# GpSimd in place of VectorE for the forward substitution in the 16x16 diagonal blocks of the RWKV mixer

## The chip, the cores and the metric

The kernel runs on one core of a Trainium2 chip. The metric is the device time of one execution in microseconds; the time of a version is the median of its runs.

## What is computed

The program runs a first block of three mixers side by side (HGRN2, mLSTM, RWKV7) over 16 meta tokens and 256 tokens of width 2048, and then two layers of a second block. The change lies in the RWKV7 mixer. For each of its 16 heads and each chunk of tokens the reference solves a unit lower triangular system:

```python
def rwkv7_chunk(s_mat, inp):
    ...
    l_ab = jnp.einsum('bhtd,bhsd,bhtsd->bhts', a_, b, d_strict)
    l_ak = jnp.einsum('bhtd,bhsd,bhtsd->bhts', a_, k, d_strict)
    rhs = (jnp.einsum('bhtd,bhdv->bhtv', a_ * jnp.exp(cw_prev), s_mat)
           + jnp.einsum('bhts,bhsv->bhtv', l_ak, v))
    u = lax.linalg.triangular_solve(jnp.eye(length, dtype=rhs.dtype) - l_ab, rhs,
                                    left_side=True, lower=True, unit_diagonal=True)
    ...
    y = (jnp.einsum('bhtd,bhdv->bhtv', r * jnp.exp(cw), s_mat)
         + jnp.einsum('bhts,bhsv->bhtv', r_b, u) + jnp.einsum('bhts,bhsv->bhtv', r_k, v))
```

## The kernel before

**Projections.** Most of the work is the product of the tokens (128 features by up to 272 tokens a tile) with all weight matrices. The helper `unit` streams a weight in pieces of 128 rows by 8 x 128 columns: SyncE's queue issues the DMA into `wraw`; ScalarE rounds the piece to `whi` (L267, by `act`); VectorE makes the remainder `wlo` = `wraw` - `whi` (L270, by `tt`); TensorE runs 24 matmuls into the PSUM tile `pj` (L291): for each of eight sub-tiles `xh` by `whi`, `xl` by `whi` and `xh` by `wlo`. There are four buffers each of `wraw`, `whi` and `wlo` (`self.nraw, self.nhl = 4, 4`), and a buffer is free when its 24 matmuls are done.

**Mixers beside the projections.** The mixers' own work is emitted beside the projections that follow, and has its matmuls in PSUM tiles named `mx`. Each engine runs its instructions in one fixed order; the framework's scheduler sets that order from its own estimates when the program is built (`schedule_with_timeline_sim=True`). What an engine's queue holds behind a waiting instruction waits too.

**The inverse of I - L.** RWKV has four groups of four heads (`front_c`, `back_c`), near 90, 315, 540 and 760 us. In a group:

- TensorE forms `Lb` (for two chunks of 128 tokens) and `Dc` (the meta tokens' part); `base_start` cuts the 16x16 diagonal blocks out of `Lb` on GpSimd (tiles `db`, `Dc`), writes them to memory (`ld`, L621) and reads them back as `LB` (L622), so that each of the 128 partitions holds a row's own block. Both DMAs are issued from GpSimd's queue.
- TensorE computes `vm,Lm` (a matmul of `vm` and `Lm`), ScalarE copies it to `rum`.
- `base_solve` solves all the small blocks at once: `yc` starts as the identity, and 15 steps each multiply a row of `LB` with a column of `yc` into `yt` and add `yt` to `yc`. The operands have 12 x 15 elements per partition in the first step and 12 x 1 in the last; 30 instructions, each of which needs the one before.
- The first reader of `yc` on TensorE is the matmul `rum,yc` (four instructions in the order, eight in the trace). The first on VectorE is `Y<-yc`, with which `inverse` begins for each chunk.

The step in the loop of `base_solve`, on VectorE:

```python
            self.mul(t, self.LB[:, j, :, j + 1:], y[:, :, j:j + 1].to_broadcast([P, 12, 15 - j]))
            self.add(y[:, :, j + 1:], y[:, :, j + 1:], t)
```

Of the kernel before, what the change touches and what calls it, by code (L numbers as in the profile page):

```python
# [13 lines left out]
ALU = mybir.AluOpType  # L14
PSUM = bass.MemoryType.PSUM
DRAM = bass.MemoryType.DRAM

P = 128
# [11 lines left out]
# ---------------------------------------------------------------- host layout  # L30
# [7 lines left out]
def unit_list():  # L38
    """(name, source, width, [(dst column, source column, count)]) in the order the weights are used."""
    u = []  # L40

    def win(name, base, i):
        u.append((f"{name}{i}", "w_in", 256, [(0, W_IN[base] + 256 * i, 256)]))

    u.append(("c_small", "w_in", 164, [(0, W_IN["c_wd"], 128), (128, W_IN["b_ig"], 4), (160, W_IN["b_fg"], 4)]))
    for g in range(4):
        for n in ("c_k", "c_r", "c_v", "c_z"):
            win(n, n, g)
    for g in range(4):
        for n in ("a_f", "a_i", "a_q", "a_z"):  # L50
            win(n, n, g)
    for j in range(8):
        win("g_c", "g_c", j)
        u.append((f"br_c{j}", "w_br2", 256, [(0, 256 * j, 256)]))
    for g in range(2):
        win("b_k", "b_k", g)
        win("b_q", "b_q", g)
        for h in (2 * g, 2 * g + 1):
            for n in ("b_v", "b_o", "b_z"):
                win(n, n, h)  # L60
    for b, s in (("a", "w_br0"), ("b", "w_br1")):
        for j in range(8):
            win(f"g_{b}", f"g_{b}", j)
            u.append((f"br_{b}{j}", s, 256, [(0, 256 * j, 256)]))
    for j in range(8):
        u.append((f"out{j}", "w_out", 256, [(0, 256 * j, 256)]))
    for l in range(2):
        def w2(name, cols, width=256):
            u.append((f"L{l}{name}", f"w_in_2_{l}", width, cols))

        w2("small", [(0, W_IN2["dt"], 32), (32, W_IN2["i_w"], 16), (64, W_IN2["i_k"], 64)], 128)
        w2("a_k", [(0, W_IN2["a_k"], 256)])
        w2("a_v", [(0, W_IN2["a_v"], 256)])
        for j in range(4):
            w2(f"i_q{j}", [(0, W_IN2["i_q"] + 256 * j, 256)])
        for j in range(4):
            w2(f"a_q{j}", [(0, W_IN2["a_q"] + 256 * j, 256)])
        for j in range(4):
            w2(f"a_g{j}", [(0, W_IN2["a_g"] + 256 * j, 256)])
        for g in range(4):  # L80
            w2(f"bc{g}", [(0, W_IN2["bm"] + 128 * g, 128), (128, W_IN2["cm"] + 128 * g, 128)])
            for j in range(2):
                w2(f"xs{2 * g + j}", [(0, W_IN2["xs"] + 512 * g + 256 * j, 256)])
            for j in range(2):
                w2(f"z{2 * g + j}", [(0, W_IN2["z"] + 512 * g + 256 * j, 256)])
        for g in range(4):
            w2(f"pool_v{g}", [(0, W_IN2["pool_v"] + 256 * g, 256)])
            w2(f"pool_g{g}", [(0, W_IN2["pool_g"] + 256 * g, 256)])
        for j in range(8):
            u.append((f"L{l}out{j}", f"w_out_2_{l}", 256, [(0, 256 * j, 256)]))  # L90
    return u
# [12 lines left out]
# per-feature vectors, feature-major: name -> (columns of 128 features)  # L104
# [73 lines left out]
def pack(inp):  # L178
    """Lays the inputs out: weights in the order of their use, vectors feature-major."""
# [58 lines left out]
# ---------------------------------------------------------------- kernel  # L238
class Kernel:
# [5 lines left out]
    # ---- helpers  # L245
# [55 lines left out]
    # ---- weights against the token matrix  # L301
    def unit(self, name, src, cols, evac, chunks=None):
        """evac(j, ps): ps [128, N] = 128 columns of the weight, transposed, times the tokens cols of src (a function of
        the tile and cols that gives the two parts); chunks: the parts of the weight's rows that meet its tiles."""
# [34 lines left out]
    def hot(self):  # L339
        """what frees the PSUM of the projections goes first"""  # L340
        return self.tc.high_priority(offset=self.hprio)
# [13 lines left out]
    def run(self, gen):  # L355
        """Emits a generator and those that it spawns together, each ahead by its own clock."""
# [15 lines left out]
    def early(self, *shape, rows=P, name="r"):  # L372
        """The same, taken now: a slot is taken at the first write, and later ones wait for it."""
        t = f = self.reg(*shape, rows=rows, name=name)
        for _ in shape[1:]:
            f = f[:, 0]
        self.G.memset(f[:, :1], 0.0)
        return t

    def reg(self, *shape, rows=P, name="r"):  # L380
        """A slot of the register file: fp32, at most 544 elements per partition."""
# [15 lines left out]
    def warm_ln(self, late):  # L397
        """has the table of the logarithm loaded before a sum that is waited for; late is what comes just before"""
        self.act(self.warm, late, AF.Ln, scale=0.0, bias=self.eps(2))

    def rstd(self, out, ssum, scale, eps):
        """out = (ssum * scale + eps) ** -0.5"""
# [3 lines left out]
    def follow(self, a, b):  # L406
        """b comes after a in the order of their engine"""
# [3 lines left out]
    # ---- program  # L411
# [37 lines left out]
    def block1(self, b1):  # L449
        nc, tc = self.nc, self.tc  # L450
        xh, xl = self.xh, self.xl
        # the tokens times the weights of the norm; the factors of the norm itself follow the projections
# [27 lines left out]
    def mixers(self, order):  # L480
        """The projections in the given order; the rest of each group runs beside those that follow."""
# [19 lines left out]
    def block1_main(self):  # L501
# [9 lines left out]
        # w_out and the residual, and what the second block's projections take (without its tokens' factors R)  # L511
# [58 lines left out]
    def residual0(self):  # L570
        """the second block's input"""
# [7 lines left out]
    def merge(self, b, y, acc, first):  # L579
        """acc += 2 sigmoid(gate) * (y @ w_br)"""  # L580
# [18 lines left out]
    # ---- RWKV7  # L599
    def lerp(self, out, ps, col):  # L600
        """out = ps + (prev - ps) * mu along the tokens"""
# [8 lines left out]
    def base_start(self, Lb):  # L610
        """the diagonal blocks of 16 of the two chunks' Lb, next to those of the meta tokens, to each of their rows"""
# [13 lines left out]
    def base_solve(self):  # L625
        """rows of ((I - L)^-1)^T in those blocks: 4 heads of each chunk, then of the meta tokens"""
# [3 lines left out]
        for j in range(15):  # L630
            t = tmp[j % 2][:, :, j + 1:]
            self.mul(t, self.LB[:, j, :, j + 1:], y[:, :, j:j + 1].to_broadcast([P, 12, 15 - j]))
            self.add(y[:, :, j + 1:], y[:, :, j + 1:], t)
# [3 lines left out]
    def inverse(self, LT, yc):  # L637
        """Y = ((I - Lm)^-1)^T for four heads; LT [s, 4, t] = Lm^T, strictly upper; yc [s, 4, 16]: Y's diagonal blocks.
        Blocks of twice the size at each level: the lower left of the lower triangular X = Y^T gains X L X."""
# [31 lines left out]
        # blocks of 64 from those of 32; X's second half is not needed any more  # L671
# [33 lines left out]
    def pair(self, K, Q, c, mask, name):  # L705
        """(head i = 2 hh + j sits on the partitions rr of feature tile j)"""
# [11 lines left out]
    def pairm(self, out, K, Q):  # L718
        """the same for the meta tokens"""
# [35 lines left out]
    def front_c(self, g):  # L755
# [7 lines left out]
        # decay and rate  # L763
# [11 lines left out]
        # sums of the decay over each chunk (times -CC is the log)  # L775
# [19 lines left out]
        # S' = exp(cref) S over the chunks  # L795
# [33 lines left out]
        # scaled operands  # L829
# [14 lines left out]
        # token-major b, k  # L844
# [27 lines left out]
        # bonus  # L872
# [9 lines left out]
        # token-major v  # L882
# [17 lines left out]
    def back_c(self, g, ops):  # L900
# [6 lines left out]
        # meta tokens: the state they leave  # L907
# [72 lines left out]
        # layer norm over each head, bonus, gate  # L980
# [17 lines left out]
    # ---- HGRN2  # L998
    def start_a(self):
        p1, P8 = self.p1, [P, 8]  # L1000
        # lower bound of the forget gate: cumsum(softmax over layers) - its first, one layer
# [57 lines left out]
    def back_a(self, g, ops):  # L1059
# [6 lines left out]
        # meta tokens: the state they leave  # L1066
# [20 lines left out]
        # first chunk: the state it leaves  # L1087
# [19 lines left out]
        # scores [s, t]: the diagonal, then pairs by the block where they part, the decay taken from its middle  # L1107
# [64 lines left out]
    # ---- mLSTM  # L1172
    def log1pexp(self, x, rows, n, alloc):
        """log(1 + exp(-|x|)) by its series in e / (2 + e)"""
# [13 lines left out]
    def conv(self, out, ps, off, taps, n, bias=None):  # L1188
        """out[t] = bias + sum_i taps[i] ps[off + t + i - 3], zero before ps"""
# [9 lines left out]
    def silu2(self, t, x):  # L1199
        """x = 2 silu(x) (or into t, for x in PSUM)"""  # L1200
# [77 lines left out]
    def back_b(self, h, k, q, vT, vm, z):  # L1278
# [4 lines left out]
        # log weights [s, t], then the scores  # L1283
# [45 lines left out]
        # layer norm over the head's 256 features  # L1329
# [19 lines left out]
    # ---- block 2  # L1349
    def layer(self, l):  # L1350
# [17 lines left out]
        # w_out: first the SSD features, then pool and attention  # L1368
# [81 lines left out]
    def nrm(self, out, ps, cols=slice(0, T)):  # L1450
        """a projection's result times its tokens' factors"""
        self.mul(out, ps, self.R[:, cols])

    def small2(self):
# [3 lines left out]
        if l == 0:  # L1458
            # halved taps and bias, so that tanh of the convolution is that of its half
# [28 lines left out]
    def back_dt(self, x):  # L1488
        reg, l, nc = self.early, self.l, self.nc
        sm = lambda *shape, name, rows=P: self.p2.tile([rows, *shape], F32, tag="d_" + name, name=name, bufs=1)  # L1490
        # dt, its log decay, and the sums over each chunk: blocks of 16, then the blocks
# [23 lines left out]
        # token-major: [token, chunk, head]  # L1515
# [17 lines left out]
    def rope(self, tmp, x, kind, o, n):  # L1533
        """x (one tile of features, tokens o .. o + n) turned by its position, in place; tmp is zero outside the rows"""
# [15 lines left out]
    def attention(self):  # L1550
# [5 lines left out]
        for j in range(4):  # L1556
# [3 lines left out]
            # each head's two parts above each other  # L1560
# [6 lines left out]
            if j == 0:  # L1567
                # index weights, token-major
# [41 lines left out]
    def back_index(self, qi, ng):  # L1610
        """index scores and the mask of the chosen keys"""
# [107 lines left out]
    def back_ssd(self, g, bc, xs, zs):  # L1719
# [19 lines left out]
        # token-major x dt, and the states after the first two chunks  # L1739
# [127 lines left out]
# ---------------------------------------------------------------- launch  # L1867
# [20 lines left out]
```

## Time and profile before

| | |
|---|---|
| median of three runs | 3028.24 us (3027.68 to 3031.04) |
| span of the profiled execution | 3026.2 us |
| TensorE matmul | 2943.5 us busy (97%) |
| VectorE | 2011.9 us (66%) |
| ScalarE | 1426.1 us (47%) |
| GpSimd | 175.8 us (6%) |

The profiled execution is known by its span; it lies 2.0 us under the median of the timed runs. A group name such as `pj<-xh,whi` gives the tile that is written and those that are read. A busy TensorE is not TensorE at its peak: matmuls are pipelined, so their durations overlap, and the distance from start to start tells the pace. An idle time in brackets lies just before the instruction, with what ended it.

### The profile page before, as it was taken

The page shows a single profiled execution, that of the slowest core. Times are in us where ns is not written, and L with a number is a line of the kernel's source. Part 1 is how long each engine was busy: PE and PEld are TensorE (multiplying, and loading weights), DVE is VectorE, ACT ScalarE, POOL GpSimd, SP SyncE. Part 2 cuts the span into 40 slices and gives each one's busy share as a digit, 9 for nine tenths or more (in the row PEclk, how much of TensorE's full clock was granted, in tenths as well). Part 3 has the DMA queues.
Part 4 walks back from the last instruction along what each step waited for, and adds up shares of the span by engine and source line. Part 5 has one row for each costly group of instructions (what it writes and reads, how often), then busy time and mean ns, then how long its engine had stood idle before and what let it go on. Part 6 is the DMA issues. An engine that isn't in the chain of part 4 may idle for free. (4 is left out here: it accounts for less than half of the span.)

```text
span 3026.2 us, 57135 instructions
## 1 busy us (share of the span) xinstructions
PE 2943.5 (97%) x23566; PEld 2824.0 (93%) x23566; DVE 2011.9 (66%) x3505; ACT 1426.1 (47%) x2041; POOL 175.8 (6%) x324
## 2 busy tenths in 40 slices
PE   8899899899899999999999999999989999999997
PEld 8899899888889999999999899999979999999997
DVE  7657657647545555566976787774568767887655
ACT  6445445435335444456544444443555444544453
POOL 1000100001000000000200000000022000000000
PEclk9999999999999999999999999999989999999999
DMA  6533433433524655556655445555545544555563
GB/s 215 148 109 110 140 105 112 140 99 126 153 91 147 187 183 187 184 186 212 193 167 163 139 152 161 167 177 176 177 158 168 178 152 152 177 174 189 175 183 124
DMA packets 134005, 479.37 MB, mean 158 GB/s; under 512 B 17552, under 2 KB 18064, under 8 KB 133232
## 3 DMA queue, kind: packets, MB, share of 16 engines
q1 hardware_dynamic: 122112, 441.80, 46.8%
q0 software_dynamic: 11200, 32.84, 3.9%
q8 instruction: 184, 3.01, 0.4%
q10 hardware_dynamic: 432, 1.09, 0.1%
q14 instruction: 77, 0.63, 0.1%
HBM read 467.35 MB, written 7.02 MB: 157 GB/s over the span
## 5 line engine op out<-in xcount | busy, mean ns | idle before, releaser
L291 PE MATMUL pj<-xh,whi 128*128 128x272 f32 (+2 forms) x6080 | 1757.7, 289 | 17.1 <-ACT xh L267 15.0
L291 PE MATMUL pj<-xh,wlo 128*128 128x272 f32 (+2 forms) x6080 | 1752.1, 288 | 16.5 <-DVE wlo L270 16.5
L291 PE MATMUL pj<-xl,whi 128*128 128x272 f32 (+2 forms) x6080 | 1749.3, 288 | 7.5 <-DVE xl L288 7.5
L267 ACT ACTIVATE whi<-wraw 128x1024 fp32r<-128x1024 f32 x840 | 887.5, 1057 | 1272.4 <-PE pj L291 1078.3
L270 DVE TENSOR_TENSOR wlo<-wraw,whi 128x1024 fp32r<-128x1024 f32 x840 | 1027.9, 1224 | 558.4 <-ACT whi L267 551.9
L291 PEld LDWEIGHTS pj<-xh,wlo 128*128 128x128 f32 x6080 | 1152.7, 190 | 29.2 <-DVE wlo L270 17.0
L291 PEld LDWEIGHTS pj<-xh,whi 128*128 128x128 f32 x6080 | 1149.0, 189 | 31.0 <-ACT xh L267 15.7
L291 PEld LDWEIGHTS pj<-xl,whi 128*128 128x128 f32 x6080 | 1151.3, 189 | 16.6 <-DVE xl L288 8.7
L291 PE MATMUL pj<-yh,wlo 128*128 128x256 f32 x384 | 108.2, 282 | 0.0
L291 PE MATMUL pj<-yh,whi 128*128 128x256 f32 x384 | 108.0, 281 | 0.0
L291 PE MATMUL pj<-yl,whi 128*128 128x256 f32 x384 | 107.9, 281 | 0.0
L267 ACT ACT_TABLE_LOAD x77 | 98.8, 1283 | 15.4 <-DVE lf L270 12.4
L291 PE MATMUL pj<-mh,wlo 128*128 128x256 f32 x256 | 73.0, 285 | 0.0
L291 PE MATMUL pj<-mh,whi 128*128 128x256 f32 x256 | 72.8, 285 | 0.0
L291 PE MATMUL pj<-ml,whi 128*128 128x256 f32 x256 | 72.6, 284 | 0.0
L291 PEld LDWEIGHTS pj<-yl,whi 128*128 128x128 f32 x384 | 72.5, 189 | 0.0
L291 PEld LDWEIGHTS pj<-yh,wlo 128*128 128x128 f32 x384 | 72.3, 188 | 0.0
L291 PEld LDWEIGHTS pj<-yh,whi 128*128 128x128 f32 x384 | 72.3, 188 | 0.0
L288 DVE SCALAR_TENSOR_TENSOR cx<-ct,hcw,cx 128x271 f32<-128x271 f32 (+2 forms) x144 | 64.2, 491 | 0.0
L270 DVE TENSOR_TENSOR yt<-LB,yc 128x180 f32<-128x180 f32 (+14 forms) x60 | 15.2, 253 | 56.2 <-DMA LB<-ld 55.3
L291 PEld LDWEIGHTS pj<-ml,whi 128*128 128x128 f32 x256 | 49.1, 192 | 0.0
L291 PEld LDWEIGHTS pj<-mh,whi 128*128 128x128 f32 x256 | 49.1, 192 | 0.0
(494 smaller groups left out, 2683.8 us busy)
## 6 DMA issues: line engine op xcount, KB each, us to landing
wraw<-in_w_dram SPq DMA_DIRECT2D x838, 512.0 KB, 3.5
L<-csd POOLq DMA_DIRECT2D x32, 256.0 KB, 4.9
LB<-ld POOLq DMA_DIRECT2D x4, 1440.0 KB, 18.6
h<-in_xt_dram POOLq DMA_DIRECT2D x8, 272.0 KB, 7.8
h<-hd POOLq DMA_DIRECT2D x8, 272.0 KB, 4.0
hd<-h POOLq DMA_DIRECT2D x8, 272.0 KB, 2.3
res<-in_xt_dram POOLq DMA_DIRECT2D x8, 256.0 KB, 4.1
hd<-acc POOLq DMA_DIRECT2D x8, 256.0 KB, 2.9
```

Of the source, the lines that this page charges most:

```text
L267: return self.S.activation(out, in_, func, **kw)
L270: return (eng or self.V).tensor_tensor(out=out, in0=a, in1=b, op=op)
L288: return self.V.scalar_tensor_tensor(out=out, in0=a, scalar=s, in1=b, op0=op0, op1=op1)
L291: return self.PE.matmul(out, lhsT, rhs, start=start, stop=stop)
```

## The change

The two instructions of each step are issued on GpSimd (`self.G`). Beside that only comments and docstrings fall away.

```diff
     def base_solve(self):
         ...
         for j in range(15):
             t = tmp[j % 2][:, :, j + 1:]
-            self.mul(t, self.LB[:, j, :, j + 1:], y[:, :, j:j + 1].to_broadcast([P, 12, 15 - j]))
-            self.add(y[:, :, j + 1:], y[:, :, j + 1:], t)
+            self.tt(t, self.LB[:, j, :, j + 1:], y[:, :, j:j + 1].to_broadcast([P, 12, 15 - j]), ALU.mult, self.G)
+            self.tt(y[:, :, j + 1:], y[:, :, j + 1:], t, ALU.add, self.G)
             yield 0.3
         return y
```

The scheduler sets a new order with it, from the first step of the substitution to about the end of the fourth group; from then on TensorE's order is the same row for row, and SyncE's is the same throughout.

VectorE in the first RWKV group, before, from the last instruction ahead of the substitution (`lp` belongs to the mLSTM mixer):

```order
L270 TENSOR_TENSOR wlo_1216<-wraw_1214,whi_1215 128x1024
L285 TENSOR_SCALAR lp1_1034<-lp0_1033 4x272
L270 TENSOR_TENSOR yt_1027<-LB_299,yc_1025 128x12x15
L1179 RECIPROCAL lp1_1034<-lp1_1034 4x272
L270 TENSOR_TENSOR yc_1025<-yc_1025,yt_1027 128x12x15
L270 TENSOR_TENSOR wlo_1246<-wraw_1244,whi_1245 128x1024
```

The same place after:

```order
L270 TENSOR_TENSOR wlo_1216<-wraw_1214,whi_1215 128x1024
L285 TENSOR_SCALAR lp1_1034<-lp0_1033 4x272
L1179 RECIPROCAL lp1_1034<-lp1_1034 4x272
L270 TENSOR_TENSOR wlo_1246<-wraw_1244,whi_1245 128x1024
L270 TENSOR_TENSOR lp1_1034<-lp1_1034,lp0_1033 4x272
L270 TENSOR_TENSOR lp0_1033<-lp1_1034 4x272
```

The reader of `LB` is gone from between the two `wlo`; `Y<-yc` is now the first instruction of VectorE that needs the solution, behind 32 instructions of `wlo` counted from the program's start where it was behind 36.

TensorE at the matmul `rum,yc` of the first group, before:

```order
L291 MATMUL pj_1560<-xh_69,wlo_1563 128x256
L291 MATMUL pj_1560<-xh_69,whi_1562 128x256
L291 MATMUL mx_1275<-rum_1023,yc_1025 16x64 x4
L291 MATMUL pj_1560<-xl_70,whi_1562 128x256
L291 MATMUL pj_1560<-xh_69,wlo_1563 128x256
```

The same place after:

```order
L291 MATMUL pj_1282<-xl_70,whi_1338 128x272
L291 MATMUL pj_1282<-xh_69,wlo_1339 128x272
L295 MATMUL mx_1185<-c0_66,c1_1061 128x4
L291 MATMUL mx_1275<-rum_1023,yc_1025 16x64 x4
L291 MATMUL pj_1282<-xh_69,whi_1338 128x272
L291 MATMUL pj_1282<-xl_70,whi_1338 128x272
```

`rum,yc` has moved forward among the projections: between it and `vm,Lm`, which keeps its place in the first group, stood 286 projection matmuls and now stand 150. In the other three groups the numbers are 221 and 145, 219 and 152, 236 and 169.

GpSimd behind the DMAs of the first group, before:

```order
L622 DMA LB_299<-ld_821 128x1x2880
L628 COPY yc_1025<-c1_156 128x192
L377 MEMSET yt_1027 128x1
L377 MEMSET yt_1029 128x1
L377 MEMSET X_1326 128x1
```

The same place after:

```order
L622 DMA LB_299<-ld_821 128x1x2880
L628 COPY yc_1025<-c1_156 128x192
L377 MEMSET yt_1027 128x1
L377 MEMSET yt_1029 128x1
L270 TENSOR_TENSOR yt_1027<-LB_299,yc_1025 128x12x15
L270 TENSOR_TENSOR yc_1025<-yc_1025,yt_1027 128x12x15
L270 TENSOR_TENSOR yt_1029<-LB_299,yc_1025 128x12x14
```

The 30 steps stand in one row behind the memsets of `yt`, with nothing between them; the memsets of the tiles for `inverse` (`X` and others) follow.

## Rows read from the trace of the kernel before

**Rows 1.** The page, busy us (share of the span) and instructions of TensorE.

```profile
PE 2943.5 (97%) x23566; PEld 2824.0 (93%) x23566; DVE 2011.9 (66%) x3505; ACT 1426.1 (47%) x2041; POOL 175.8 (6%) x324
```

**Rows 2.** Who waited, TensorE: us in total, times, longest us.

```profile
PE pj L291 <- DVE wlo L270: 16.5, 2, 8.8
...
PE mx L291 <- DVE att L1140: 10.5, 2, 10.0
...
PE mx L291 <- DVE E L270: 7.3, 1, 7.3
```

**Rows 3.** By stretches, TensorE: length, busy us, granted clock, DMA share, GB/s; sum.

```profile
80.00:130.00 50.00, 38.39 (x278) 0.86 0.54 147
315.00:345.00 30.00, 19.96 (x156) 0.83 0.52 125
...
sum 150.00, PE 112.92; mean PE 28.23
```

**Rows 4.** By stretches, TensorE in the five half-clock stretches up to 800 us; sum.

```profile
103.33:113.57 10.24, 6.04 (x26) 0.50 0.35 103
123.80:127.20 3.40, 3.40 (x18) 0.50 0.65 220
...
553.89:560.71 6.82, 4.24 (x25) 0.50 0.34 90
...
sum 40.94, PE 23.27; mean PE 4.65
```

**Rows 5.** Timeline of VectorE, each group's first reader of `LB`: start us, duration us.

```profile
104.05 0.35 DVE L270 TENSOR_TENSOR yt<-LB,yc 128x180 f32<-128x180 f32 x1 [15.88 <-DMA LB<-ld]
...
333.27 0.35 DVE L270 TENSOR_TENSOR yt<-LB,yc 128x180 f32<-128x180 f32 x1 [12.25 <-DMA LB<-ld]
...
553.64 0.35 DVE L270 TENSOR_TENSOR yt<-LB,yc 128x180 f32<-128x180 f32 x1 [13.08 <-DMA LB<-ld]
...
777.86 0.34 DVE L270 TENSOR_TENSOR yt<-LB,yc 128x180 f32<-128x180 f32 x1 [14.12 <-DMA LB<-ld]
```

**Rows 6.** By tile (`yt`, `yc`, `LB`): duration ns min/median/max; the landing of `LB`.

```profile
L270 DVE TENSOR_TENSOR yt<-LB,yc x60: 177/254/347, 104.0 to 796.2; 128x180 f32<-128x180 f32 x4, 128x168 f32<-128x168 f32 x4, 128x156 f32<-128x156 f32 x4, 128x144 f32<-128x144 f32 x4
L270 DVE TENSOR_TENSOR yc<-yc,yt x60: 178/249/338, 106.1 to 796.4; 128x180 f32<-128x180 f32 x4, 128x168 f32<-128x168 f32 x4, 128x156 f32<-128x156 f32 x4, 128x144 f32<-128x144 f32 x4
...
DMA to landing us min/median/max: 17.2/18.6/19.5
```

**Rows 7.** Timeline of TensorE: `vm,Lm`; first and last of 97 projection matmuls.

```profile
85.62 0.62 PE L291 MATMUL mx<-vm,Lm 16*16 16x64 f32 x8
86.39 0.29 PE L291 MATMUL pj<-xl,whi 128*128 128x272 f32 x1
...
98.42 0.28 PE L291 MATMUL pj<-xl,whi 128*128 128x272 f32 x1
...
315.39 0.61 PE L291 MATMUL mx<-vm,Lm 16*16 16x64 f32 x8
...
538.10 0.62 PE L291 MATMUL mx<-vm,Lm 16*16 16x64 f32 x8
...
757.60 0.62 PE L291 MATMUL mx<-vm,Lm 16*16 16x64 f32 x8
```

**Rows 8.** GpSimd's 128x64 steps, by tile and by form: durations in ns.

```profile
L270 POOL TENSOR_TENSOR Dc<-db x8: 318/448/1302, 79.3 to 754.0; 128x64 f32<-128x64 f32 x8
...
L270 POOL TENSOR_TENSOR Dc<-db 128x64 f32<-128x64 f32 x8 | 5.7, 727 | 0.2
```

**Rows 9.** Timeline of GpSimd, steps in a row and a 128x256 step.

```profile
308.88 1.52 POOL L270 TENSOR_TENSOR db<-db 128x256 f32<-128x256 f32 x2
310.48 0.38 POOL L270 TENSOR_TENSOR Dc<-db 128x64 f32<-128x64 f32 x1
...
650.09 0.73 POOL L270 TENSOR_TENSOR den<-y 128x256 f32<-128x256 f32 x1 [10.83 <-DVE y L270]
```

**Rows 10.** By stretches, landing to `Y<-yc`, busy us: PE, PEld, DVE, ACT, POOL.

```profile
104.05:137.87 33.82, 27.56 (x191) 27.19 (x192) 30.73 (x76) 14.96 (x19) 0.10 (x1) 0.81 0.50 149
```

## The prediction

> **What bounds the kernel now.** I read the page's busy shares first. TensorE is busy for 2943.5 of 3026.2 us, so about 83 us in which it stands still are all that an edit off TensorE can win directly, besides stretches at half clock [rows 1]. The table of who waited for whom on TensorE came next: its longest waits are on VectorE, for `wlo` (the low part of a weight tile) and for `att` and `E` (operands of the HGRN2 mixer) [rows 2]. A table by stretches places them. Around the four RWKV groups, near 100, 330, 555 and 780 us, TensorE is busy for 112.92 of 150 us, so 37.1 us are idle, and the clock is lowered as well, to a mean of 0.86 and 0.83 of full speed in the first two [rows 3]. In the five stretches of the first 800 us in which the clock is granted at half (0.50, the 1.2 GHz level), TensorE is busy for 23.27 us [rows 4]; the same work at the full level (2.4 GHz) takes half of that, which makes 11.6 us more lost. **The four groups thus cost 37.1 + 11.6 = 48.7 us.**
>
> VectorE's timeline gives the cause. The first step of the substitution, `yt<-LB,yc`, waits 15.88 us in VectorE's queue at 88 us and 12.25, 13.08 and 14.12 us in the other groups, each time for the DMA that brings `LB` [rows 5]. The queue is in order. Every `wlo` behind that step waits as well, and TensorE stops when its four buffered weight tiles are used up: its last projection matmul starts at 98.42 us, 10 us after VectorE fell idle at 88.2 us [rows 5, 7], and the next waits 8.8 us for `wlo` [rows 2]. The table by tile gives a median of 18.6 us from issue to landing of this DMA [rows 6]. The mixer's own matmuls are no cause: `rum,yc`, the first that reads the solution, comes long after.
>
> **The change part by part.** 30 instructions in each of four groups, with medians of 254 and 249 ns [rows 6], leave VectorE: about 30 us of an engine that does not set the end, so worth nothing by itself. What counts is which queue holds the wait, and where the reader of the solution stands.
>
> First, what it removes. On VectorE nothing is left in front of `wlo` that waits for `LB`. The 48.7 us go if nothing takes their place.
>
> Second, what it adds. GpSimd now waits for `LB`. Behind that stand only one-element memsets of later tiles and the next group's `db`, which is hundreds of microseconds away, and the DMAs on GpSimd's queue come before; I cost this at nothing.
>
> Third, what it moves. TensorE's `rum,yc` stood 286, 221, 219 and 236 projection matmuls behind `vm,Lm`, and now stands 150, 145, 152 and 169 behind it, by counting the order. That is the term that decides. `vm,Lm` starts at 85.62, 315.39, 538.10 and 757.60 us and takes 0.6 [rows 7]. A 272-column projection matmul takes 12.03 us / 96 = 0.125 us from start to start [rows 7]; 80 and 96 of those in groups three and four have 260 columns, which by columns is 0.12. In groups two and three three sets of eight small HGRN2 matmuls lie between, estimated at the 0.62 of `vm,Lm`: 1.9. TensorE would come to `rum,yc` at
>
> - 85.62 + 0.6 + 150 x 0.125 = 105.0 us
> - 315.39 + 0.6 + 145 x 0.125 + 1.9 = 336.0
> - 538.10 + 0.6 + 72 x 0.125 + 80 x 0.12 + 1.9 = 559.2
> - 757.60 + 0.6 + 73 x 0.125 + 96 x 0.12 = 778.8
>
> `LB` lands, by the start of its first reader, at 104.05, 333.27, 553.64 and 777.86 [rows 5]: 0.9, 2.7, 5.6 and 0.9 us earlier, 10.1 us in sum. So GpSimd has hardly begun when TensorE asks, and **TensorE stands for the rest of the chain of 30 dependent steps**. `rum,yc` is in TensorE's in-order queue, so the projections behind it wait too, though their weight tiles are ready.
>
> The chain's price has no row. On GpSimd a 128x64 step takes 0.318 at the least [rows 8] and 128x256 takes 0.73 [rows 9]; the line between them gives 0.18 + 0.00215 per element. The steps have 180, 168, ... 12 elements, on average 96: 0.39. One step follows the other by 0.08 (a pair that starts at 308.88 and takes 1.52 ends at 310.40, its successor starts at 310.48) [rows 9]. 30 x 0.47 = 14.0 us undisturbed. Beside a busy VectorE it is dearer: the 128x64 steps average 0.727, with one of 1.302, so 0.41 above the least [rows 8]; all 30 steps at that would make 14.0 + 12.3 = 26.3 us. The low end is the row of 64 elements for every step without a gap, 30 x 0.318 = 9.5. I take 16.5. VectorE's work between the landing and `Y<-yc` was 30.7 us [rows 10], less 30 steps (7.6) and four `wlo` that now stand behind `Y` (4.9) makes 18.2, and it starts at 88 instead of 104. With some waits it is over near 110, so about the first six steps are disturbed: 14.0 + 6 x 0.41 = 16.5.
>
> TensorE's new idle time is 4 x 16.5 - 10.1 = 55.9 us. The clock follows: after stops of 7 to 10 us it fell to the lower level in each group and came back 4 to 6 us after TensorE had resumed, with 4.24 to 6.04 us of work in it, 23.27 - 3.40 = 19.9 in all four [rows 4]. I take half of that again, 9.9 us, and leave out the fifth piece, of 3.40 us, which belongs to the backlog that the first stop left on VectorE. New loss 65.8, old loss 48.7: **17.1 us slower.** From about 870 us on, TensorE's order is row for row the same, so nothing is given back later.
>
> The rule that speaks here concerns the two engines' shared access. The steps of GpSimd that lie beside VectorE's two-input subtractions are the long ones [rows 8]. The Trainium skill, "SBUF — State Buffer", section "Who interferes with whom", says that a VectorE instruction with two SBUF inputs and a GpSimd instruction that reads SBUF exclude each other for a whole instruction. The trace agrees: 1.302 against 0.318 us. By the rule each step could have to wait for one of VectorE's, which is the first rival; by the sum above VectorE runs dry early.
>
> **The rivals.** *Disturbed throughout.* VectorE keeps finding work while GpSimd solves, in the range of 20 to 26.3 us a chain. At the end: 4 x 26.3 - 10.1 + 9.9 - 48.7 = 56.3 us slower, 3084.5. For it: base_start's 128x64 steps average twice their least. Against it: VectorE's queue now meets `Y<-yc` soon after and must wait there as well. Chance 0.20.
>
> *A draw.* The old stop goes, the new one is just as long. The break-even chain is (48.7 + 10.1 - 9.9) / 4 = 12.2 us, 0.41 a step; with the undisturbed 14.0 it is still 7 us slower. For it: the small steps may be cheaper than the line. Chance 0.10, 3028.
>
> *Faster.* The steps cost a flat 0.318 or less, gap included, because most are smaller than any that the trace has: 4 x 9.5 - 10.1 + 9.9 - 48.7 = 10.9 us faster, 3017. It decides from 10.7 us a chain on (0.2% of the time). Against it: 0.318 is the least of eight. Chance 0.12.
>
> *No effect.* TensorE is stopped by the DMA itself, not by VectorE's order, and stands as long as before. The rows speak against it: the waiting matmuls read `wlo`, `att` and `E`, none of which needs `LB` [rows 2]. It is in the draw's chance.
>
> **How the numbers follow.** The profiled execution has a span of 3026.2 us, 2.0 under the median of 3028.24; I add the difference to the median: 3028.24 + 17.1 = 3045.3. The forecast (chains of 13 to 20 us, 3031 to 3059) has 0.58. Slower by over 0.2% (6 us, about what a measurement of this kernel can tell from no change): forecast 0.58 + disturbed 0.20 = 0.78; same 0.10; faster 0.12. The range takes in the draw and most of the disturbed case: 3026 to 3076.
>
> **What would show it.** VectorE's idle time in front of `yt` is gone and TensorE has no wait on `wlo` near 100 us. TensorE has four waits of 11 to 16 us in front of `rum,yc`, put down to GpSimd's `yc`; half clock follows each. GpSimd's 30 steps take 14 to 20 us from the landing. Wrong would be: a chain under 12 us, TensorE that comes to `rum,yc` later than worked out because it starves elsewhere, or the four waits on another name.

## The result, and the profile after

The changed kernel takes 3054.45 us (median of four runs, 3053.20 to 3055.46) beside 3028.93 us for the kernel before on the same chip (four runs, 3027.68 to 3031.04): a ratio of 1.01 with a 95% interval of 1.0088 to 1.0113. On a second chip it was 3055.81 beside 3025.47 us, 1.0095 (1.0080 to 1.0110). The profiled execution has a span of 3053.3 us, 27.1 more than that of before. The forecast was 17.1 us slower.

The page of the changed kernel, busy us; beside [rows 1] TensorE is busy for 7.7 us less in a span that is 27.1 us longer, so it is idle for 34.8 us more:

```profile
PE 2935.8 (96%) x23566; PEld 2818.3 (92%) x23566; DVE 1998.9 (65%) x3385; ACT 1426.4 (47%) x2041; POOL 236.0 (8%) x444
```

Who waited, TensorE after: us in total, times, longest us, to be held against [rows 2]. The waits for `wlo` are gone. Four new ones stand in front of `rum,yc`; `yc`, `Y` and `X` are all GpSimd's end of the chain, since the memsets of `Y` and `X` stand right behind the last step in its queue.

```profile
PE mx L291 <- POOL yc L270: 19.7, 1, 19.7
PE mx L291 <- POOL Y L377: 19.4, 2, 12.6
PE mx L291 <- POOL X L377: 16.7, 1, 16.7
...
PE mx L291 <- DVE att L1140: 8.4, 1, 8.4
PE mx L295 <- DVE c L270: 6.9, 1, 6.9
```

TensorE's timeline after, start us, duration us, in brackets the idle time before. Where [rows 7] had the projections run on behind `vm,Lm`, TensorE now stands at `rum,yc`, and in the first two groups at one more place:

```profile
84.07 0.62 PE L291 MATMUL mx<-vm,Lm 16*16 16x64 f32 x8
...
110.58 0.26 PE L295 MATMUL mx<-c,c 4*128 4x4 f32 x1 [6.91 <-DVE c L270]
...
123.48 1.03 PE L291 MATMUL mx<-rum,yc 16*16 16x64 f32 x8 [12.64 <-POOL Y L377]
...
342.46 0.63 PE L291 MATMUL mx<-E 128*32 128x32 f32 x8 [8.43 <-DVE att L1140]
...
354.45 1.03 PE L291 MATMUL mx<-rum,yc 16*16 16x64 f32 x8 [6.76 <-POOL Y L377]
...
584.26 1.03 PE L291 MATMUL mx<-rum,yc 16*16 16x64 f32 x8 [16.73 <-POOL X L377]
...
818.34 1.03 PE L291 MATMUL mx<-rum,yc 16*16 16x64 f32 x8 [19.73 <-POOL yc L270]
```

Stretches around the four groups, TensorE after: length, busy us, granted clock, DMA share, GB/s. 71.2 us idle, where [rows 3] gave 37.1:

```profile
80.00:140.00 60.00, 40.45 (x314) 0.80 0.50 126
315.00:365.00 50.00, 34.81 (x271) 0.86 0.53 127
535.00:600.00 65.00, 48.27 (x401) 0.87 0.49 126
775.00:835.00 60.00, 40.27 (x321) 0.83 0.50 129
sum 235.00, PE 163.81; mean PE 40.95
```

The half-clock stretches after, same columns; the sum of TensorE's work in them is 30.25 us, beside 23.27 in [rows 4]:

```profile
107.22:131.11 23.89, 7.89 (x40) 0.50 0.21 70
...
803.53:824.01 20.48, 5.67 (x29) 0.50 0.24 80
sum 78.50, PE 30.25; mean PE 5.04
```

GpSimd's first and last step in the first group, then the first step of the other groups, as [rows 5] had them on VectorE. The chain lasts from 105.51 to 123.43 us: 17.92, and 17.45, 16.72 and 16.43 in the others.

```profile
105.51 0.50 POOL L270 TENSOR_TENSOR yt<-LB,yc 128x180 f32<-128x180 f32 x1 [20.36 <-DMA LB<-ld]
...
109.98 2.07 POOL L270 TENSOR_TENSOR yc<-yc,yt 128x156 f32<-128x156 f32 x1
...
123.20 0.23 POOL L270 TENSOR_TENSOR yc<-yc,yt 128x12 f32<-128x12 f32 x1
...
336.95 0.50 POOL L270 TENSOR_TENSOR yt<-LB,yc 128x180 f32<-128x180 f32 x1 [21.12 <-DMA LB<-ld]
...
567.48 0.50 POOL L270 TENSOR_TENSOR yt<-LB,yc 128x180 f32<-128x180 f32 x1 [19.35 <-DMA LB<-ld]
...
801.85 0.50 POOL L270 TENSOR_TENSOR yt<-LB,yc 128x180 f32<-128x180 f32 x1 [21.07 <-DMA LB<-ld]
```

The transfer of `LB` itself takes longer than in [rows 6], 21.6 us in the median instead of 18.6:

```profile
DMA to landing us min/median/max: 20.2/21.6/22.2
```

And the weights wait beside it. ScalarE's timeline after, where a `whi` waits for its weight piece:

```profile
105.27 2.15 ACT L267 ACTIVATE whi<-wraw 128x1024 fp32r<-128x1024 f32 x2 [10.40 <-DMA wraw<-in_w_dram]
...
337.08 1.06 ACT L267 ACTIVATE whi<-wraw 128x1024 fp32r<-128x1024 f32 x1 [11.73 <-DMA wraw<-in_w_dram]
```

Before, there was one such wait of note, in the first group:

```profile
103.86 1.06 ACT L267 ACTIVATE whi<-wraw 128x1024 fp32r<-128x1024 f32 x1 [7.45 <-DMA wraw<-in_w_dram]
```

After, the other two groups have 9.38 and 10.78 us; these waits end at 567.64 and 801.96 us, when TensorE already stands at `rum,yc` (from 567.5 and 798.6 us on). In the first two groups they end in the stops at `c,c` and `E` (VectorE's `wlo` waits for that `whi`, and the small work behind it in VectorE's queue waits too).

### The profile page after: what moved, and what is told of

The parts are those of the page before. It is cut to its first block, busy times and chain, and to the rows that moved or that the text cites. A ratio compares the mean times of both kernels' runs of the same rounds, so it can differ in the third digit from the quotient of the medians.

```text
span 3053.3 us, 57125 instructions
## 1 busy us (share of the span) xinstructions
PE 2935.8 (96%) x23566; PEld 2818.3 (92%) x23566; DVE 1998.9 (65%) x3385; ACT 1426.4 (47%) x2041; POOL 236.0 (8%) x444
## 5 line engine op out<-in xcount | busy, mean ns | idle before, releaser
L291 PEld LDWEIGHTS pj<-xh,whi 128*128 128x128 f32 x6080 | 1148.9, 189 | 32.8 <-ACT xh L267 15.5
L291 PE MATMUL mx<-rum,yc 16*16 16x64 f32 x32 | 4.1, 306 | 55.9 <-POOL yc L270 19.7
## 6 DMA issues: line engine op xcount, KB each, us to landing
LB<-ld POOLq DMA_DIRECT2D x4, 1440.0 KB, 21.6
```

The costliest lines, as they stand in the source:

```text
L291: return self.PE.matmul(out, lhsT, rhs, start=start, stop=stop)
```

## Experiments

Where several runs stand beside one kernel before, the ratio is given with its 95% interval. One table first, made in one way for every run from its profiled execution: TensorE's idle time in the stretches 80 to 164, 308 to 380, 530 to 614 and 750 to 846 us; its busy time at the half clock up to 900 us; then idle + half of that, and the span, both less those of the kernel before.

| kernel | idle us | half-clock work us | loss against before | span against before | time, ratio to before on its chip |
|---|---|---|---|---|---|
| before | 37.1 | 33.5 | 0 | 0 (3026.2) | |
| after | 71.9 | 30.2 | +33.2 | +27.1 | 1.01 (1.0088 to 1.0113) |
| after, second chip (e8) | 71.4 | 32.8 | +34.0 | +27.7 | 1.0095 (1.0080 to 1.0110) |
| e1, late place | 22.2 | 22.8 | -20.2 | -20.5 | 0.9941 (0.9922 to 0.9959) |
| e2, small `LB` | 16.1 | 30.1 | -22.7 | -28.4 | 2999.5 beside 3023.4 us, one run |
| e3, half the chain | 44.5 | 34.5 | +7.9 | +7.6 | 3035.5 beside 3023.4, one run |
| e4, before with the late place | 39.4 | 40.3 | +5.7 | +5.3 | 3033.3 beside 3023.4, one run |
| e5, later still | 16.0 | 26.2 | -24.8 | -24.1 | 0.9927 (0.9912 to 0.9942) |
| e6, e5 with small `LB` | 8.6 | 21.6 | -34.4 | -32.1 | 0.9894 (0.9879 to 0.9909) |
| e7, VectorE held back | 18.7 | 39.5 | -15.4 | -13.6 | 0.9954 (0.9936 to 0.9972) |
| e9, between | 43.3 | 36.1 | +7.5 | +6.8 | 1.0043 (1.0026 to 1.0059) |
| e10, before, wide `LB` | 15.0 | 13.0 | -32.3 | -31.2 | 0.9923 (0.9906 to 0.9940) |
| e11, after, wide `LB` | 40.7 | 34.0 | +3.9 | -1.2 | 1.0001 (0.9991 to 1.0010) |
| e12, late place, wide `LB` | 2.0 | 3.4 | -50.2 | -48.2 | 0.9852 (0.9838 to 0.9867) |

The two columns of differences agree within 2.3 us in nine of the thirteen rows, so the stretches around the four groups hold nearly the whole matter. In the other four (the changed kernel, its repeat, e2 and e11, all with `rum,yc` at the early place) the span is 5 to 6 us better than the account. The traces show where these lie: in four groups of RWKV's small matmuls (`RT,KT`, `AT,BT`, `ru,Y` and `RT,BT`, 64 of each). Added up from each one's start to the next matmul's, without stops, they take 30.2 us before, 23.4 to 23.8 in these four kernels and 28.4 to 30.5 in all others, e3 included. Of the 256, 78 start within 0.03 us of the matmul that follows in each of these four kernels, and 50 in the kernel before: the scheduler's new order has put them next to each other in another way.

Half is a round figure for what the lower clock costs: 256-column projection matmuls follow each other by 0.21 us at half clock and by 0.12 at full. And timed executions of the kernel before lie anywhere from 3017.38 to 3031.04 us, so the span against its one profiled execution is the rougher measure, and the ratios the firmer one.

**e1: where TensorE meets the solution.** `npjc` counts the weight pieces whose projections have been emitted; when it reaches the number in `hold`, `rum,yc` is ordered behind that piece's last matmul, and `Y<-yc` (in the same way) behind its `wlo`. The steps stay on GpSimd.

```diff
         self.act(ru, pu3)
+        hold = [self.npjc + 13, [], []]
         base = yield from self.base_solve()
+        self.held.append(hold)
...
-            self.mm(pu3[:, i], Ym[:, i], ru[:, i])
+            hold[1].append(self.mm(pu3[:, i], Ym[:, i], ru[:, i]))
```

> The changed kernel, with the matmul rum,yc and the VectorE instruction Y<-yc tied in order behind a projection 13 weight pieces after vm,Lm (312, 268, 272 and 310 projection matmuls in the four groups instead of 150, 145, 152 and 169). Theory: TensorE stood for the solution (71 us of idle time around the four groups and about 13 us of half clock). The solution was ready 39.4, 37.8, 38.1 and 41.1 us after vm,Lm; TensorE would come 39.6, 36, 36 and 38.5 us after it, so about 7 us of stops stay: some 75 us less than the changed kernel, near 2978. Rival 1, the DMA of LB delays the weight pieces so that TensorE runs dry anyway: about 7 us of stop a group stay, put down to wlo or whi, with half clock: near 3015. Rival 2, GpSimd beside VectorE is what costs: no difference to 3054.

Measured 3006.2 us (six runs) beside 3023.35: faster than both kernels. The four stops of 12.64, 6.76, 16.73 and 19.73 us became none, 4.69, 4.99 and 2.32. It gained about 48 us on the changed kernel, where 75 were expected. The chain grew, since VectorE runs on now: GpSimd's 30 steps took 22.7, 20.2, 21.4 and 22.5 us, and 12.0 us of stops stay at `rum,yc` instead of 7. The stop at `c,c` in the first group stays too, with 5.99 us, 22.8 us of work still run at half clock, and the small matmuls' 6 us are lost again.

**e2: the transfer cut to a fifteenth**, with `rum,yc` 6, 6, 6 and 7 pieces behind `vm,Lm`, as in the changed kernel:

```diff
-        self.nc.gpsimd.dma_start(self.LB.rearrange("p s a b -> p (s a b)"),
-                                 ld[:, :15 * 192].unsqueeze(1).to_broadcast([8, 16, 15 * 192]))
+        self.nc.gpsimd.dma_start(self.LB[:, :1].rearrange("p s a b -> p (s a b)"),
+                                 ld[:, :192].unsqueeze(1).to_broadcast([8, 16, 192]))
```

> The changed kernel, with a DMA of LB of 1/15 of the bytes (the first of 15 rows; the others are zero, so this leaves out most of the substitution's values, not its instructions), rum,yc kept at 150, 144, 144 and 165 projection matmuls. Theory: LB lands about 3 us after its issue instead of 21; the chain of 17 us then ends about 20 to 23 us after vm,Lm, and TensorE comes 19.4 to 21: stops of 0 to 3 us a group, 2975 to 2990. Rival 2 (disturbance between the engines): 3054, since all GpSimd steps are still there.

Measured 2999.5 us, 10 above the expected range. `LB` lands after 3.3 us, no `whi` waits longer than 2.0 us for its weight piece, and the stops at `rum,yc` shrink to 6.54, 1.52, 3.45 and 4.58 us; they don't vanish, since the chain again lasts 19 to 22.5 us.

**e3: half the chain**, at the same places:

```diff
-        for j in range(15):
+        for j in range(0, 15, 2):
```

> The changed kernel with 8 of the 15 steps (16 instructions instead of 30; the rest of the substitution is left out), rum,yc kept at 144, 144, 144 and 168 projection matmuls. Theory: the chain is on TensorE's path one to one; it falls from 17 to about 9 us, so each of the four stops is 8 us shorter: 32 us less, some more for the clock, 3015 to 3024. Rival 1 (TensorE waits for data that the DMA delays): 3054.

Measured 3035.5 us, missed by 12. The chains take 11.5, 10.8, 9.9 and 10.0 us, 26 us less in sum, and the idle time falls by 27.4 (71.9 to 44.5): about one to one, as the theory has it. At `rum,yc` itself the stops fall only from 55.9 to 43.8 us; the other 15.3 us are the stops at `c,c` and `E`, which are gone, for the scheduler's order differs here beside the edit. The span falls by 19.5 only; half-clock work takes 2 of the difference, and the small matmuls, which take 28.9 us here and 23.4 in the changed kernel, 5.

**e4: the late place alone**: the edit of e1 in the kernel before, with the substitution on VectorE.

> The kernel before, with its substitution on VectorE, and rum,yc and Y<-yc held back as in the first run (312, 268, 272, 310 projection matmuls behind vm,Lm). Theory: the stop of before comes from the first step that waits for LB in VectorE's queue, not from rum,yc, so nothing is won: 3022 to 3035, TensorE still waits on wlo, att or E. If the place of rum,yc alone were the gain of the first run, this would gain as well (below 3000).

Measured 3033.3 us. The waits on `wlo` (8.15 and 6.61 us), `att` (10.46) and `E` (9.49) are all still there, so the place of `rum,yc` earns nothing as long as VectorE holds the wait for `LB`.

**e5 and e9: other places**: the edit of e1 with 15 in place of 13, and with 10, 9, 9 and 9 in the four groups.

> The changed kernel with rum,yc (and the first Y<-yc) put still later in the order, 360, 316, 320 and 358 projection matmuls behind vm,Lm in the four groups (the run e1_later13 had the matmul about two weight pieces earlier). My theory (TensorE stands because it meets the solution before GpSimd has finished): e1_later13 still had stops of 4.69, 4.99 and 2.32 us in front of rum,yc in groups two to four and half clock behind them; two pieces are 5 to 6 us, so these three stops go and the time falls by 12 to 20 us more, to about 0.987 to 0.990 of the kernel before. The stop of 6 us at 111 us in group one, where weight pieces arrive late beside the LB transfer, stays. Rival (the transfer of LB is what stops TensorE): the three stops turn up again under another name (wlo, pj) and the time stays at 0.994.

> The changed kernel with rum,yc 240, 198, 216 and 213 projection matmuls behind vm,Lm in the four groups, between the changed kernel (150, 145, 152, 169) and e1_later13 (312, 268, 272, 310); the first Y<-yc goes with it. If TensorE's stop is simply the end of GpSimd's chain less the time at which TensorE's order reaches rum,yc, then from e1_later13 (stops of 0, 4.69, 4.99 and 2.32) 70, 56, 56 and 97 matmuls at 0.125 us (twice that where the clock is at half) make stops of 7 to 14 us longer, less 3 us of a chain that VectorE disturbs less: about 6, 10, 9 and 11 us, 36 in sum, beside the 6 us in group one that late weight pieces cost. That is about the idle time of the kernel before: within 0.4% of it, between the 1.0095 of the changed kernel and the 0.994 of e1_later13. If the place did not matter in proportion (a threshold in the weight transfers, say), the time is that of one of its two neighbours.

e9: 1.0043, at the edge of the expected 0.4%, with stops of 3.04, 9.00, 10.44 and 12.02 us at `rum,yc` (expected 6, 10, 9, 11). e5: no stop over 0.3 us there. In the order of the place (about 150, 215, 290 and 340 matmuls behind `vm,Lm`) the idle time is 71.9, 43.3, 22.2 and 16.0 us: the stop is the end of the chain less TensorE's arrival. Past the end of the chain a later place gives little more: e5 gained 0.14% on e1 and not the 0.4 to 0.7% expected, since of the 12 us that e1 still lost at `rum,yc` half came back as small waits (for `X`, `whi`, `wlo`) and some as half-clock work.

**e6: e5 with the small transfer of e2.**

> The same late places, and the transfer of LB cut to a fifteenth (one row of the blocks in place of 15, the rest of the tile is zero; most of the substitution's values are left out, all its 30 steps stay). This takes away what is left: the weight pieces that arrive late in group one. My theory: 6 us of stop and about 3 us of half clock go, so 8 to 12 us under e5_later15. If the late weight pieces had another cause, it is equal to e5_later15.

8.8 us under e5, as expected: the stop of 6.10 us at `c,c` in the first group is gone. But the clock falls all the same. TensorE in e6's half-clock stretches, and its timeline ahead of the first one:

```profile
133.41:140.24 6.83, 6.05 (x29) 0.50 0.23 79
348.45:355.28 6.83, 6.41 (x30) 0.50 0.20 73
570.32:573.73 3.41, 3.41 (x18) 0.50 0.12 46
781.95:788.77 6.82, 5.75 (x27) 0.50 0.26 79
```

```profile
130.61 0.27 PE L291 MATMUL pj<-xh,wlo 128*128 128x256 f32 x1
130.81 0.61 PE L291 MATMUL mx<-rum,yc 16*16 16x64 f32 x8
132.18 0.32 PE L291 MATMUL mx<-um,bkm 16*64 16x64 f32 x2 [0.75 <-ACT um L267]
```

Full projections up to 130.8 us, then only the mixer's small matmuls, with a wait of 0.75 us among them, and at 133.41 the granted clock is 0.50. A long stop is not needed for it.

**e7: the substitution back on VectorE, its first step behind four, two, four and three more `wlo`** in the four groups than in the kernel before, with `rum,yc` and `Y<-yc` at the places of e5:

```diff
+        first = [self.npjc + 8, [], []]         # beside hold, for the first step
...
-            self.mul(t, self.LB[:, j, :, j + 1:], y[:, :, j:j + 1].to_broadcast([P, 12, 15 - j]))
+            m = self.mul(t, self.LB[:, j, :, j + 1:], y[:, :, j:j + 1].to_broadcast([P, 12, 15 - j]))
+            first[2] += [m] if j == 0 else []
```

> The kernel before (substitution on VectorE), with its first step put four weight pieces later in VectorE's queue (behind 29 wlo in place of 25 in group one, and likewise in the others) and rum,yc and Y<-yc at the same places as in e5_later15; TensorE's order is the one of e5_later15, only the engine of the 30 steps differs. My theory (what cost time before was the wait for LB in VectorE's queue, and after the wait for the solution in TensorE's, and the engine itself matters little): LB has landed when VectorE comes to it, the wait of 12 to 16 us falls under 4, and the time is within 6 us of e5_later15. Rival (GpSimd is needed, because 30 us of steps on VectorE are in the way of wlo): VectorE's steps hold up wlo by 8 us a group and it is 10 to 30 us slower than e5_later15.

0.9954, about 10 us behind e5, at the border of the two expectations. VectorE's first step waits no more in the first and fourth group, but still 8.80 and 9.04 us in the other two, where VectorE comes to it before `LB` has landed. Of the 10.5 us between the two spans 2.7 are idle time and 6.7 the clock, 3.4 of these from a stretch at 517.63 to 524.46 us. No stop explains it: TensorE is busy for 19.22 of 20 us from 510 to 530 us, with that stretch in it, and in e5 for 19.21 of 20 from 505 to 525 us, at full clock throughout. Whether GpSimd is the better place once the order is right is therefore not settled; that VectorE alone gets more than half of e5's gain is.

**e8: the changed kernel again**, beside the others of its chip.

> The changed kernel as it is, on the same chip as the others, so that they stand beside it: 25 us over the kernel before, with stops in front of rum,yc that add up to 50 to 60 us.

It repeats the first result: 1.0095, with stops of 13.24, 6.20, 16.5 and 20.0 us at `rum,yc`, 55.9 in sum.

**e10 to e12: the transfer itself.** While 1440 KB of `LB` take 18.6 or 21.6 us, 512 KB of a weight piece take 3.5. The traces of before and after point to the reason: counting the 128 packets of 11.5 KB by their start and duration, mostly six to eight are in flight at a time, eight more often than any other number in seven of the eight transfers, and never more than ten. The source is read as 8 rows that go to 16 partitions each. So `ld` is written twice here and read as 16 rows. The Trainium skill, "DMA: Bandwidth & Descriptors", section "Why a DMA increments its semaphore by 16 and not by 1", says that a DMA runs on the largest number of engines, 16 at most, that divides the outermost size of both its sides. By that it would be 8 before the edit and 16 with it.

```diff
-        ld = self.dr.tile([8, 16 * 192], F32, tag="ld", name="ld", bufs=2)
-        self.nc.gpsimd.dma_start(ld.rearrange("b (s f) -> (b s) f", s=16), Dc.rearrange("p a b -> p (a b)"))
+        ld = self.dr.tile([8, 2, 16 * 192], F32, tag="ld", name="ld", bufs=2)
+        for t in range(2):
+            self.nc.gpsimd.dma_start(ld[:, t].rearrange("b (s f) -> b s f", s=16), Dc.rearrange("p a b -> p (a b)"))
         self.nc.gpsimd.dma_start(self.LB.rearrange("p s a b -> p (s a b)"),
-                                 ld[:, :15 * 192].unsqueeze(1).to_broadcast([8, 16, 15 * 192]))
+                                 ld.rearrange("b t f -> (b t) f")[:, :15 * 192].unsqueeze(1).to_broadcast([16, 8, 15 * 192]))
```

> The kernel before with only the transfer of LB changed: ld is written twice (two rows of the source in place of one, by a second small DMA) and read as 16 rows of which each goes to 8 partitions, in place of 8 rows that go to 16 partitions each. The orders of TensorE and VectorE stay as before. In the traces of before and after never more than 8 or 9 of the 11.5 KB packets of LB are in flight at a time, eight over most of the transfer, while weight pieces fly in sixteens: the transfer seems to use half of the 16 DMA engines. My theory: it takes all 16 now and its data part of 15 us is halved, so it lands 10 to 13 us after issue in place of 18.6; VectorE's wait for it (55.3 us in sum) falls to 25 to 33, TensorE's idle time in the groups from 37 to 8 to 15, and the time falls by 0.7 to 1.0%. Rival (the transfer is limited by what the DMA engines move in all, beside the weights): landing stays at 16 to 19 us and the time within 0.3% of before.

> The changed kernel with the same wider transfer; rum,yc stays where it was, 150, 147, 154 and 174 matmuls behind vm,Lm. My theory: LB lands 8 to 10 us earlier, the four stops in front of rum,yc (55.9 us in sum) shrink by that each, to 18 to 28, and the two stops of 7 and 8 us by late weight pieces go; 40 to 50 us less idle time, so from 1.0095 of the kernel before to 0.993 to 0.998. If the late weight pieces came from the sheer amount of data, those two stops stay and the time is 0.998 to 1.003 of before.

> The late places of e1_later13 (312, 268, 272 and 310 matmuls) and the wider transfer together. My theory: the chain ends before TensorE comes to rum,yc, no stop is left that LB causes, and the time is that of e6_later15_small_lb, 0.988 to 0.991 of before, with all of the substitution done. If the weights still arrive late in group one it stays at 0.991 to 0.994.

Now 15 or 16 packets in flight are the commonest number, 19 the most, and the transfer lands after 11.1, 11.6 and 12.0 us in the three kernels. A packet is no quicker (0.83 to 0.87 us in the median, 0.69 to 1.00 in the kernels before and after): there are more of them at a time. This is in keeping with that section of the Trainium skill. VectorE's wait in e10, who waited (us in total, times, longest); it was 55.3 in the kernel before:

```profile
DVE yt L270 <- DMA LB<-ld: 28.5, 4, 9.9
```

e10, the kernel before with nothing but this, is 0.9923, inside the expected 0.990 to 0.993: of the 28.5 us that VectorE still waits, TensorE stands idle for at most 15.0, and the buffered weight pieces cover the rest. e11, the changed kernel with it, is a draw with before (1.0001; expected 0.993 to 0.998, missed), and 23.7 us slower than e10, on the same chip. TensorE in e11 at `rum,yc`:

```profile
117.03 1.03 PE L291 MATMUL mx<-rum,yc 16*16 16x64 f32 x8 [12.15 <-POOL Y L377]
...
341.80 1.03 PE L291 MATMUL mx<-rum,yc 16*16 16x64 f32 x8 [10.91 <-POOL Y L377]
...
563.59 1.03 PE L291 MATMUL mx<-rum,yc 16*16 16x64 f32 x8 [8.04 <-POOL X L377]
...
788.64 1.03 PE L291 MATMUL mx<-rum,yc 16*16 16x64 f32 x8 [9.20 <-POOL yc L270]
```

The stops at `c,c` and `E` are gone, but 40.3 us stand in front of `rum,yc` (expected 18 to 28): in the first two groups TensorE now arrives 6.5 and 9.8 us earlier too, since nothing starves it on the way, and the chain of 17.2 to 18.1 us is not hidden. e12, with the late place as well, has no stop at `rum,yc` and 2.0 us idle in all four groups. It takes 2980.17 us beside 3022.69, 0.9852, better than expected and **the fastest version**: 1.5% under the kernel before, with the substitution on GpSimd and all of it computed.

## Why the prediction was right in direction and short in size

**The mechanism held.** The waits of 12 to 16 us on VectorE and of 16.5 us on `wlo` went, and four stops in front of `rum,yc` took their place, under the name that was forecast. e1, e5 and e9 show that TensorE's place in the order decides: with the same engine and the same steps the time goes from 1.0095 to 0.9927. e4 shows the other half: the place alone is worth nothing while VectorE waits.

**The chain held.** 16.5 us were taken; 17.9, 17.5, 16.7 and 16.4 were measured. Without disturbance it would be 13.6 (each step's least of the four groups, 0.50 and 0.57 us for 180 elements down to 0.23 for 12, with 0.08 between steps), forecast 14.0. Three single steps in each group took 1.3 to 2.07 us, all twelve beside a `wlo` of VectorE, which reads two tiles in SBUF; in the ten kernels with the steps on GpSimd that holds for all 215 steps over 1 us, though not every step beside a `wlo` is long. The Trainium skill, "SBUF — State Buffer", section "Who interferes with whom", says that such a VectorE instruction contends with a GpSimd instruction that reads SBUF; this trace agrees. The reason given, that VectorE would run dry, was right, if later than forecast: in the first group it has work beside the chain until 117.1 us, in the fourth nothing from 807.2 until `Y<-yc` at 818.4. Where it does not run dry (e1, e5, e6, e12) the chain takes 20 to 24 us. The rival "disturbed throughout" had the right price, for other kernels than this one.

**TensorE's arrival held where nothing starved it.** From the start of `vm,Lm` to the beginning of the stop it took 21.4 us in the third and fourth group, forecast 21.1 and 21.2. In the first two it took 26.8 and 31.1, forecast 19.4 and 20.6, because of the stops of 6.91 and 8.43 us.

**The step that failed is the landing of `LB`.** The sum took the landing times over from the trace before, 18.4, 17.9, 15.5 and 20.3 us behind the start of `vm,Lm`. Measured were 21.4, 20.3, 21.3 and 24.6: 15.6 us more in the four. Some 11.9 of these are the transfer itself, from issue to landing; the rest comes from the third group, where `LB` was issued 0.95 us behind the start of `vm,Lm` and not 3.15 ahead of it. Before, VectorE's standstill slowed the weight stream too: 992 to 1496 KB of weights moved while an `LB` was under way, and 1772 to 2120 KB after. A packet of `LB` took 0.69 to 0.74 us in the median of a transfer before and 0.93 to 1.00 after, with as many in flight. The DMA share by stretches in the first group before (length, VectorE's busy us, granted clock, DMA share, GB/s):

```profile
84.00:92.00 8.00, 3.00 (x4) 1.00 0.73 171
92.00:96.00 4.00, 0.00 (x0) 1.00 0.60 131
96.00:100.00 4.00, 0.00 (x0) 1.00 0.49 131
100.00:104.00 4.00, 0.00 (x0) 0.92 0.28 74
```

The same after:

```profile
84.00:92.00 8.00, 6.11 (x10) 1.00 0.85 184
92.00:96.00 4.00, 3.85 (x6) 1.00 1.02 179
96.00:100.00 4.00, 1.33 (x4) 1.00 1.00 174
100.00:104.00 4.00, 0.00 (x0) 1.00 0.49 125
```

A DMA share of 1.00 and 1.02 from 92 to 100 us, weights and `LB` both late, and VectorE empty in the end, for want of weights. So the forecast idle time of 55.9 us plus 15.6 of landing plus 2.5 of chain makes 74.0; measured are 71.2 to 71.9. That the stops at `rum,yc` alone add up to 55.86, as forecast, is chance: the two starving stops took the extra time in the first two groups.

The rival "no effect" (the DMA itself stops TensorE) was put aside too quickly: `wlo`, `att` and `E` don't read `LB`, but the weights that they wait behind share the DMA with it. Two runs show that part: the small transfer takes 9 us off e5 (e6), and with the wide one the stops at `c,c` and `E`, 15.3 us in the changed kernel, are gone (e11). How much of the loss of the kernel before it is stays open, since e10 shortens VectorE's wait for `LB` and the traffic together.

**The clock was wrong in its cause.** 9.9 us were taken for the new half-clock work, 15.1 measured (half of 30.25); two stretches that the kernel before has at 864 and 888 us (10.2 us of work, 5.1 lost), left out as not part of the groups, went away with the change. The two errors nearly cancel. The first of the two stretches, with TensorE busy throughout:

```profile
864.50:871.33 6.83, 6.83 (x23) 0.50 0.17 65
```

But half clock was treated as the consequence of a long stop, and up to 900 us e6 has four such stretches without one, e12 a single short one.

**The account.** Idle time and clock give 33.2 us (the table); the spans 27.1, the medians 25.5 and 30.3. The landing's 15.6 us are about what the account has over the forecast of 17.1. The 6 us that it has over the span are a term that the sum doesn't hold: the new order moved more than `rum,yc`, and RWKV's small matmuls take 6.8 us less in it.

## What to carry to other kernels

When a waiting step moves to another engine, ask which in-order queue the wait lands in, and how much work is buffered for the engine behind it. VectorE had four weight pieces ahead of TensorE; TensorE's own queue has nothing, so each microsecond of the chain there counted. A landing time read from a kernel in which the weight stream had slowed down is too early for one in which it runs on: other transfers come back with it. And before a wait for a transfer is moved around, count how many of its packets are in flight.

## What the runs showed of the hardware

- A DMA whose source has 8 outer rows kept mostly six to eight packets in flight, ten at most, and needed 18.6 to 21.6 us for 1440 KB; with 16 rows, 15 or 16 in flight most often, it needed 11.1 to 12.0 (all in the median). Beside the narrow one ScalarE waited 9.4 to 11.7 us for a weight piece of 512 KB in each group of the changed kernel; such pieces land after 3.5 us in the median.
- GpSimd's dependent two-input fp32 steps cost 0.23 us (12 elements per partition) to 0.57 us (180) plus 0.08 between them; beside VectorE's two-input `wlo` single steps take up to 2.07 us in the changed kernel.
- The granted clock of TensorE fell to 0.50 not only after stops: in the kernel before it did at 864.50 us, behind mixer matmuls without a stop, and stayed there for 6.83 us in which TensorE was busy throughout.
